# Hybrid trunk, attention stage: the rest of a pair's query and key projection is asked for one head sooner in the order

## The chip, the cores and the metric

One core of a Trainium2 chip runs the whole program. The metric is the device time of one execution in microseconds (us). The kernel before takes 1062.12 us (median of 3 runs, 1062.06 to 1062.16). The profile comes from an execution of its own, with its own time.

## The reference

Two residual layers on 512 tokens of width 1024, all in float32. Each has a mixer and then an MLP, with an RMSNorm ahead of both; a last norm ends it.

```
h = x
layer 0:  h += attention(rmsnorm(h)) @ w_o        # 16 heads of 64, 8 chunks of 64 tokens
          h += relu(rmsnorm(h) @ w1)**2 @ w2      # hidden 4096
layer 1:  h += recurrent_block(rmsnorm(h))        # conv, gates, linear scan
          h += relu(rmsnorm(h) @ w1)**2 @ w2
out = rmsnorm(h) * norm_final

attention: q, k, v = h @ w_qkv
           s = q @ k.T / 8 + bias[head][clip(i - j)]     # own chunk and the 8 before it
           o = softmax(s) @ v
```

The change touches the attention of layer 0 alone. With 512 tokens the band of nine chunks covers all earlier tokens, so scores are computed in four blocks of 128 queries against 128, 256, 384 and 512 keys.

## The kernel before, in words

*Precision.* Every product of two float32 matrices is done as three matmuls of rounded parts (`mm3`): the operand is split into a high part, a copy in the narrower format, and a low part, the operand minus that copy; high x high, high x low and low x high are added. So each weight tile that is loaded (`wr`) costs a copy on ScalarE (`wh`, line 140) and a subtraction on VectorE (`wl`, line 143) before TensorE can use it.

*Weights.* `plan` lists every weight tile in the order of use. `want(n)` hands out the next n and asks for loads up to four tiles ahead. Five split tiles can be alive at once, three raw ones. All loads go through SP's queue.

*Attention.* The heads are worked in pairs, pair p being heads 2p and 2p+1. The projections of pairs 0 and 1 come first, with the norm. The rest is done head by head in the loop of line 539: in iteration i the scores of head i (`score`, tile `s` on lines 408 and 409, eight matmuls), the transposes of head i-1's probabilities (`turn`, tile `x`, line 439, ten), and the weighing of values of head i-2 (`weigh`, tile `oa`, lines 454 and 455, eight). Between a head's scores and its transposes lies its softmax: on VectorE the addition of the bias with a maximum (line 412), on ScalarE the exponentials (line 419), on VectorE a reciprocal and the scaling (lines 423 and 426).

*Projection steps as filling.* The projections of the later pairs (`q2`, `k2`, ... `q7`, `k7`), the values (`v0`, `v1`) and the output projection (`wo...`) stand in one queue of generators, in this order: v0, q2, k2, q3, k3, q4, k4, v1, q5, k5, q6, k6, q7, k7, then the output projection. One step is three matmuls (one `mm3`) and costs two credits. `fill(7.6)` gives 7.6 credits, with at most 3 kept from before, and runs steps while the credit is above zero; it stands behind `score`, behind `turn` and behind `weigh`. An item may only start in a fill once a certain head's scores have been written (for pair p, head 2p-3). `need(name)` runs steps until the named item is finished, whatever the credit, which may fall far below zero; later fills then do nothing until it is paid back.

At the end of an item stands its output. For a key projection this is `k_out`: a scaling on VectorE (tile `tk`, line 316), then for each head of the pair a copy on ScalarE (`kh`, line 321), a subtraction on VectorE (`kl`, line 322) and two small DMAs on SP's queue that copy both to the other 64 partitions (lines 323 and 324), since the scores multiply the low and the high part of a query in one matmul. `q_out` (lines 304 to 312) is alike without the DMAs.

*Buffers.* Eight PSUM banks: four with the tag "mm" (projections, `oa`), four with the tag "at", of which a head's scores take three and a head's transposes three. Query and key tiles have two buffers per head of a pair, so that pair p+2 reuses those of pair p. The bias of four heads (`bias_of`, line 295) has one buffer: its load on SP's queue (line 297), four copies and a fill on POOL (lines 299 and 300).

*Order.* The source gives no order per engine. The framework that builds the program takes the source's order as the rank of each instruction, estimates when its operands and its buffer will be there, and writes each engine's queue from that; where the higher-ranked instruction would not be ready, a later-ranked one is put ahead. On the chip every engine then runs its queue in that order and waits where an operand is late.

The lines that set the order around the change:

```
        def fill(n):
            credit[0] = min(credit[0], 3) + n
            while credit[0] > 0 and queue and at[queue[0][2][0]] >= queue[0][2][1]:
                step()

        for i in range(NH + 2):
            if i < NH:
                ...
                if i >= 4:
                    need(f"k{i // 2}")
                score(i)
```

Of the kernel before, what the change touches and what calls it, by code (L numbers as in the profile page):

```python
# [40 lines left out]
def trunk(ctx: ExitStack, tc: tile.TileContext, xT, cols, gfin, win, wqkv, wo, rwin, rga, rgx, rwo, w1, w2, out):  # L41
# [21 lines left out]
    def residual(name):  # L63
        both = [per.tile([P, 4, T], F32, name=f"{name}{i}", tag=f"hx{i}") for i in range(2)]
        hT[:] = [both[k // 4][:, k % 4] for k in range(KT)]
        hT2[:] = [both[k // 2][:, 2 * (k % 2) : 2 * (k % 2) + 2] for k in range(4)]
# [221 lines left out]
    with ExitStack() as actx:  # L288
# [6 lines left out]
        def bias_of(g):  # L295
            b = ab.tile([P, 4, T], F32, name=f"bias{g}", tag="bias")
            nc.sync.dma_start(b[:, :, 2 * P :], win[4 * g : 4 * g + 4].rearrange("h p j -> p h j"))
            for h in range(4):
                G.tensor_copy(b[:, h, 0 : 2 * P], b[:, h, 2 * P : 2 * P + 1].to_broadcast([P, 2 * P]))
            G.memset(b[0:HD, :, T - HD :], NEG)  # L300
            biases[g] = b
# [96 lines left out]
        def score(h):  # L398
            kh, kl = kk[h]
            s0, s1, s2 = atp(f"s0{h}"), atp(f"s1{h}"), atp(f"s2{h}")  # L400
            sc = [s0[:, 0:P], s0[:, P : 3 * P], s1[:, : 3 * P], s2]
            pt = a2.tile([P, 10 * P], F32, name=f"p{h}", tag="p")
            mx = a2.tile([P, 4], F32, name=f"mx{h}", tag="mx")
            sm = a2.tile([P, 4], F32, name=f"sm{h}", tag="sm")
            b = biases[h // 4]
            for t in range(4):
                n = (t + 1) * P
                PE.matmul(sc[t], q[h][:, t * P : n], kl[:, :n], start=True, stop=False)
                PE.matmul(sc[t], q[h][:, t * P : n], kh[:, :n], start=False, stop=True)  # L409
            for t in range(4):  # L410
                n = (t + 1) * P
                V.tensor_tensor_reduce(  # L412
                    out=pt[:, seg[t] : seg[t] + n], in0=sc[t], in1=b[:, h % 4, T - n :],
                    scale=1.0, scalar=-3.0e38, op0=ALU.add, op1=ALU.max, accum_out=mx[:, t : t + 1],
                )
            V.tensor_scalar(mx, mx, -1.0, None, ALU.mult)  # L416
            for t in range(4):
                n = (t + 1) * P
                S.activation(  # L419
                    pt[:, seg[t] : seg[t] + n], pt[:, seg[t] : seg[t] + n], AF.Exp,  # L420
                    bias=mx[:, t : t + 1], accum_out=sm[:, t : t + 1],
                )
            V.reciprocal(sm, sm)
            for t in range(4):
                n = (t + 1) * P
                V.tensor_scalar(pt[:, seg[t] : seg[t] + n], pt[:, seg[t] : seg[t] + n], sm[:, t : t + 1], None, ALU.mult)
            pts[h] = pt

        def turn(h):
            pt = pts.pop(h)  # L430
            x0, x1, x2 = atp(f"x0{h}"), atp(f"x1{h}"), atp(f"x2{h}")
            dst = {(0, t): (x0, t * P) for t in range(4)}
            dst.update({(1, t): (x1, (t - 1) * P) for t in range(1, 4)})
            dst.update({(2, t): (x2, (t - 2) * P) for t in range(2, 4)})
            dst[3, 3] = (x1, 3 * P)
            for kt in (0, 1, 3, 2):
                for t in range(kt, 4):
                    b, c = dst[kt, t]
                    PE.transpose(b[:, c : c + P], pt[:, seg[t] + kt * P : seg[t] + (kt + 1) * P], ident)  # L439
            pH = a2.tile([P, 10 * P], F32R, name=f"pH{h}", tag="pH")  # L440
            pL = a2.tile([P, 10 * P], F32R, name=f"pL{h}", tag="pL")
            for b, c, n in ((x0, 0, T), (x1, T, T), (x2, 2 * T, 2 * P)):
                S.copy(pH[:, c : c + n], b[:, :n])  # L443
                V.tensor_sub(pL[:, c : c + n], b[:, :n], f(pH[:, c : c + n]))
            pHL[h] = (pH, pL)

        def weigh(h):
            pH, pL = pHL.pop(h)
            p, hh = h // 2, h % 2
            oa = mmp(f"oa{h}")  # L450
            for kt in range(4):
                c, n = pseg[kt]
                vv = vt[p // 2][:, kt, p % 2, 2 * hh : 2 * hh + 2, :].rearrange("p s d -> p (s d)")
                PE.matmul(oa[:, T - n :], vv, pL[:, c : c + n], start=kt == 0, stop=False)
                PE.matmul(oa[:, T - n :], vv, pH[:, c : c + n], start=False, stop=kt == 3)
            own, oth = HALF[hh], HALF[1 - hh]
            if hh == 0:
                oT[p] = a2.tile([P, T], F32, name=f"o{p}", tag="o", bufs=1)
            ax = a2.tile([P, T], F32, name=f"ax{h}", tag="ax", bufs=1)
            S.copy(ax[own], oa[oth])  # L460
            V.tensor_add(oT[p][own], oa[own], ax[own])
            if hh == 1:
                oH = ao.tile([P, T], F32R, name=f"oH{p}", tag="oH")
                oL = ao.tile([P, T], F32R, name=f"oL{p}", tag="oL")
                S.copy(oH, oT[p])
                V.tensor_sub(oL, oT[p], f(oH))
                oHL[p] = (oH, oL)
# [54 lines left out]
        def step():  # L522
            try:
                credit[0] -= next(queue[0][1])
            except StopIteration:
                queue.pop(0)
# [6 lines that stand above are left out]
        def need(name):  # L533
            while any(name == item[0] for item in queue):
                step()
# [3 lines left out]
        for i in range(NH + 2):  # L539
            if i < NH:  # L540
                if i % 4 == 0 and i > 0:
                    bias_of(i // 4)
                if i >= 4:
                    need(f"k{i // 2}")
                score(i)
                at["s"] = i
            fill(FILL)
            if 0 <= i - 1 < NH:
                turn(i - 1)
            fill(FILL)  # L550
            if 0 <= i - 2 < NH:
                if i == 15:
                    need("woA")
                need(f"v{(i - 2) // 8}")
                weigh(i - 2)
                if i == 9:
                    residual("h")
                    for k in range(KT):
                        nc.sync.dma_start(hT[k], xT[k * P : (k + 1) * P, :])
                at["w"] = i - 2  # L560
            fill(FILL)
# [478 lines left out]
```

## Time and profile before

| | |
|---|---|
| median of 3 runs | 1062.12 us |
| the profiled execution | 1062.76 us, span of its instructions 1060.7 us |
| TensorE (PE) | 1051.2 us busy, 99% of the span, 4820 matmuls |
| weight loads (PEld), beside the matmuls | 870.6 us, 82% |
| VectorE (DVE) | 798.6 us, 75% |
| ScalarE (ACT) | 586.9 us, 55% |
| DMA | 111.51 MB, 105 GB/s on average |
| granted TensorE clock | 0.999 |

An engine's busy time is the sum of its instructions' durations. Matmuls overlap in the engine: their starts are recorded, their ends are modelled, so a matmul that is shown with 0.39 us may be followed by the next one after 0.23 us. PEld rows are weight loads, which run beside the matmul before. A row of the timeline that ends in a bracket tells how long the engine stood idle before it, and what it waited for. Tiles are named without their numbers, so `s` is the score tile of any head; which head it is follows from the order of the rows. The attention stage with its output projection lies between about 36 and 240 us.

### The profile page before, as it was taken

The numbers are of one execution on the slowest core, as the hardware profiler recorded it, in microseconds if no ns is written. First come the engines' busy times: TensorE is split into PE (matmuls) and PEld (weight loads), VectorE is DVE, ScalarE is ACT, GpSimd is POOL, SyncE is SP. The second block draws the span as 40 slices with busy tenths as digits, with TensorE's granted clock in tenths as the row PEclk, the third lists the DMA queues.
The fourth block names the chain that finished last, engine by engine and source line by source line (L and its number), as shares of the span: only waits on it lengthen the run. The fifth ranks groups of instructions, "written<-read, shape, count | busy, mean of one in ns | idle before, by whom it ended". The sixth has DMA issues, their size and how long they took to land.

```text
span 1060.7 us, 12851 instructions
## 1 busy us (share of the span) xinstructions
PE 1051.2 (99%) x4820; PEld 870.6 (82%) x4820; DVE 798.6 (75%) x1176; ACT 586.9 (55%) x888; POOL 8.8 (1%) x28
## 2 busy tenths in 40 slices
PE   9999999999999999999999999999999999999997
PEld 7888888888888888888888878888888888888886
DVE  6798779867395697587599799984387487577596
ACT  6677557645464554454456587555454454454454
POOL 0000000000000000000000000000000000000000
PEclk9999999999999999999999999999999999999999
DMA  8444353255046036026103222283136126125002
GB/s 263 117 124 135 80 168 110 70 164 164 21 121 192 6 96 202 21 80 198 40 0 118 84 77 88 71 286 92 40 87 201 31 80 198 40 79 179 1 1 80
DMA packets 128414, 111.51 MB, mean 105 GB/s; under 512 B 4321, under 2 KB 104673, under 8 KB 128353
## 3 DMA queue, kind: packets, MB, share of 16 engines
q1 hardware_dynamic: 127776, 109.99, 33.9%
q8 instruction: 38, 0.62, 0.2%
q10 hardware_dynamic: 576, 0.72, 0.2%
q14 instruction: 24, 0.19, 0.1%
HBM read 104.39 MB, written 2.10 MB: 100 GB/s over the span
## 4 chain that ended last, share of the span: by engine, by line
PE 93%; DVE 2%; DMA 2%; ACT 1%; issue 1%; SPq 0%; ACTq 0%; DVEq 0%
PE u L217 11%; PE u L219 11%; PE u L218 11%; PE x L219 5%; PE x L218 5%; PE x L217 5%; PE y L217 3%; PE y L218 3%; PE y L219 3%; PE x L439 2%; PE wo L217 1%; PE wo L218 1%; PE ro L219 1%; PE ro L217 1%; PE xb L217 1%; PE wo L219 1%
## 5 line engine op out<-in xcount | busy, mean ns | idle before, releaser
L143 DVE TENSOR_TENSOR wl<-wr,wh 128x1024 fp32r<-128x1024 f32 (+1 forms) x122 | 146.5, 1203 | 94.7 <-ACT wh L140 90.0
L140 ACT CAST wh<-b 128x1024 fp32r<-128x1024 f32 x112 | 117.8, 1052 | 177.2 <-PE u L218 130.9
L140 ACT CAST wh<-wr 128x1024 fp32r<-128x1024 f32 (+1 forms) x121 | 125.7, 1039 | 140.6 <-PE u L218 66.1
L143 DVE TENSOR_TENSOR wl<-b,wh 128x1024 fp32r<-128x1024 f32 x112 | 136.6, 1219 | 87.7 <-ACT wh L140 87.6
L217 PE MATMUL u<-hnH,wh 128*128 128x512 f32 x512 | 200.1, 391 | 0.0
L219 PE MATMUL u<-hnH,wl 128*128 128x512 f32 x512 | 199.4, 389 | 0.0
L218 PE MATMUL u<-hnL,wh 128*128 128x512 f32 x512 | 199.2, 389 | 0.0
L219 PEld LDWEIGHTS u<-hnH,wl 128*128 128x128 f32 x512 | 96.1, 188 | 20.2
L218 PEld LDWEIGHTS u<-hnL,wh 128*128 128x128 f32 x512 | 96.2, 188 | 19.8
L217 PEld LDWEIGHTS u<-hnH,wh 128*128 128x128 f32 x512 | 96.1, 188 | 19.7
L138 DVE TENSOR_TENSOR b<-b,b 128x1024 f32<-128x1024 f32 x64 | 76.3, 1216 | 1.8 <-DMA b<-in_w 1.5
L217 PE MATMUL x<-wh,h 128*128 128x512 f32 x128 | 50.0, 391 | 0.0
L218 PE MATMUL x<-wl,h 128*128 128x512 f32 x128 | 49.9, 390 | 0.0
L641 ACT ACTIVATE a<-u 128x512 f32<-128x512 f32 x64 | 37.8, 591 | 13.3 <-PE u L219 13.3
L629 DVE SCALAR_TENSOR_TENSOR d<-x,rq,d 128x512 f32<-128x512 f32 x60 | 42.8, 743 | 0.5 <-PE x L219 0.5
L642 ACT ACTIVATE a<-a 128x512 f32<-128x512 f32 x64 | 40.6, 635 | 1.8
L419 ACT ACTIVATE p<-p,mx 128x128 f32<-128x128 f32 (+1 forms) x64 | 35.2, 552 | 6.2 <-DVE mx L416 6.0
L662 ACT CAST h<-a 128x1024 fp32r<-128x1024 f32 (+2 forms) x34 | 27.2, 800 | 6.7 <-PE y L218 5.7
L412 DVE CUSTOM_DVE_ANT_0 p<-s,bias 128x128 f32<-128x128 f32 (+1 forms) x64 | 27.7, 484 | 3.4 <-PE s L409 3.1
L443 ACT CAST pH<-x 128x512 fp32r<-128x512 f32 (+1 forms) x48 | 21.7, 517 | 13.7 <-PE x L439 13.5
L218 PEld LDWEIGHTS x<-wl,h 128*128 128x128 f32 x128 | 24.0, 188 | 4.9
L217 PEld LDWEIGHTS x<-wh,h 128*128 128x128 f32 x128 | 24.0, 188 | 4.9
(342 smaller groups left out, 2290.5 us busy)
## 6 DMA issues: line engine op xcount, KB each, us to landing
wr<-in_w SPq DMA_DIRECT2D x64, 512.0 KB, 3.9
b<-in_w SPq DMA_DIRECT2D x64, 512.0 KB, 4.3
wr<-in_wqkv SPq DMA_DIRECT2D x20, 512.0 KB, 3.9
wr<-in_rwin SPq DMA_DIRECT2D x16, 512.0 KB, 3.4
wr<-in_wo SPq DMA_DIRECT2D x8, 512.0 KB, 4.0
wr<-in_rwo SPq DMA_DIRECT2D x8, 512.0 KB, 3.4
x<-in_xT SPq DMA_DIRECT2D x8, 256.0 KB, 4.6
bias<-in_win SPq DMA_DIRECT2D x4, 512.0 KB, 4.6
```

The costliest lines, as they stand in the source:

```text
L138: V.tensor_sub(raw, raws[x, half], raws[y, half])
L140: S.copy(H[:, :n], raw[:, :n])
L143: low = V.tensor_sub(L[:, :n], raw[:, :n], f(H[:, :n]))
L217: PE.matmul(acc, WH, XH, start=start, stop=False, skip_group_check=more)
L218: PE.matmul(acc, WH, XL, start=False, stop=False, skip_group_check=more)
L219: PE.matmul(acc, WL, XH, start=False, stop=stop, skip_group_check=more)
L412: V.tensor_tensor_reduce(out=pt[:, seg[t] : seg[t] + n], in0=sc[t], in1=b[:, h % 4, T - n :], scale=1.0, scalar=-3.0e38, op0=ALU.add, op1= ...
L419: S.activation(pt[:, seg[t] : seg[t] + n], pt[:, seg[t] : seg[t] + n], AF.Exp, bias=mx[:, t : t + 1], accum_out=sm[:, t : t + 1],)
L629: V.scalar_tensor_tensor(d, acc, r, d, ALU.mult, ALU.add)
L641: S.activation(c, acc.rearrange("p (h c) -> p h c", h=2), AF.Relu)
L642: S.activation(c, c, AF.Square)
L662: S.copy(H[:, ks], raw[n][:, ks])
```

## The change

In iteration i of the loop the projection of the next pair's keys (and with it everything ahead of it in the queue) is finished before the scores of an odd head already: `need` names pair (i+1)//2, from head 3 on and at most pair 7, where it named pair i//2 from head 4 on. So pair p is finished ahead of the scores of head 2p-1 and no longer ahead of those of head 2p. The steps that `need` runs spend credit, and later fills run fewer.

```
--- before.py
+++ after.py
@@ -540,8 +540,8 @@
             if i < NH:
                 if i % 4 == 0 and i > 0:
                     bias_of(i // 4)
-                if i >= 4:
-                    need(f"k{i // 2}")
+                if i >= 3:
+                    need(f"k{min((i + 1) // 2, 7)}")
                 score(i)
                 at["s"] = i
             fill(FILL)
```

## Rows read from the trace of the kernel before

**Rows 1.** The page: span, and busy time, share and instructions of TensorE.
```profile
span 1060.7 us, 12851 instructions
...
PE 1051.2 (99%) x4820; PEld 870.6 (82%) x4820; DVE 798.6 (75%) x1176; ACT 586.9 (55%) x888; POOL 8.8 (1%) x28
```

**Rows 2.** Busy time by stretch: length, each engine's us (instructions), clock, DMA share, GB/s.
```profile
36.00:60.00 24.00, 23.72 (x122) 19.52 (x121) 19.63 (x58) 17.92 (x44) 0.00 (x0) 1.00 0.30 80
60.00:100.00 40.00, 39.56 (x206) 33.29 (x204) 36.12 (x89) 26.45 (x63) 2.54 (x5) 1.00 0.45 122
100.00:160.00 60.00, 60.00 (x312) 51.17 (x311) 47.87 (x119) 36.70 (x84) 1.68 (x5) 1.00 0.46 136
160.00:240.00 80.00, 79.80 (x407) 66.47 (x405) 66.59 (x150) 48.51 (x106) 1.97 (x5) 1.00 0.38 117
300.00:400.00 100.00, 100.00 (x443) 82.78 (x442) 75.03 (x103) 51.84 (x63) 0.00 (x0) 1.00 0.35 106
```

**Rows 3.** Waits of TensorE, whole span: us in total, times, longest.
```profile
PE s L408 <- DMA kl<-kl: 0.4, 1, 0.4
PE s L408 <- DVE v L354: 0.3, 1, 0.3
```

**Rows 4.** TensorE in order of time, end of k2 to head 4's transposes.
```profile
74.77 0.39 PE L219 MATMUL qk2k_out<-hnH,wl 128*128 128x512 f32 x1
75.00 0.39 PE L217 MATMUL qk3q_out<-hnH,wh 128*128 128x512 f32 x1
75.23 0.39 PE L218 MATMUL qk3q_out<-hnL,wh 128*128 128x512 f32 x1
...
80.58 0.40 PE L218 MATMUL qk3q_out<-hnL,wh 128*128 128x512 f32 x1
81.42 0.30 PE L408 MATMUL s<-kl,q 128*128 128x128 f32 x1 [0.44 <-DMA kl<-kl]
...
82.79 1.25 PE L439 MATMUL x<-ident,p 128*128 128x128 f32 x10
83.80 0.48 PE L219 MATMUL qk3q_out<-hnH,wl 128*128 128x512 f32 x1
...
89.50 1.21 PE L439 MATMUL x<-ident,p 128*128 128x128 f32 x9
```

**Rows 5.** TensorE in order of time, end of k5 to head 10's scores.
```profile
152.30 0.39 PE L219 MATMUL qk5k_out<-hnH,wl 128*128 128x512 f32 x1
152.53 0.40 PE L454 MATMUL oa<-pL,v 128*128 128x512 f32 x1
...
153.75 0.45 PE L217 MATMUL qk6q_out<-hnH,wh 128*128 128x512 f32 x1
...
157.91 0.39 PE L217 MATMUL qk6q_out<-hnH,wh 128*128 128x512 f32 x1
158.14 0.22 PE L408 MATMUL s<-kl,q 128*128 128x128 f32 x1
```

**Rows 6.** VectorE in order of time: k2's output, first reductions of heads 4 and 12.
```profile
75.66 0.69 DVE L316 TENSOR_TENSOR tk<-qk2k_out,n0acc 128x512 f32<-128x512 f32 x1
...
78.42 1.40 DVE L322 TENSOR_TENSOR kl<-tk,kh 64x512 fp32r<-64x512 f32 x2
...
82.26 0.29 DVE L412 CUSTOM_DVE_ANT_0 p<-s,bias 128x128 f32<-128x128 f32 x1 [0.41 <-PE s L409]
...
180.17 0.28 DVE L412 CUSTOM_DVE_ANT_0 p<-s,bias 128x128 f32<-128x128 f32 x1
```

**Rows 7.** SP's issues (the bias load, k2's copies) and POOL's last bias steps, by time.
```profile
67.91 0.37 SPq L297 DMA_DIRECT2D bias<-in_win  x1
...
74.31 0.30 POOL L300 MEMSET bias<- 64x256 f32 x1
...
79.12 1.18 SPq L324 DMA_DIRECT2D kl<-kl  x2
...
169.55 0.30 POOL L300 MEMSET bias<- 64x256 f32 x1
```

**Rows 8.** Waits of ScalarE's weight splits, 36 to 216 us: total, times, longest.
```profile
ACT wh L140 <- PE qk5k_out L218: 2.5, 1, 2.5
...
ACT wh L140 <- PE qk4k_out L218: 1.7, 1, 1.7
```

**Rows 9.** Landing times of the four bias loads, from issue.
```profile
DMA to landing us min/median/max: 3.7/4.6/6.2
```

More of the change, by code (lines that the diff above doesn't have):

```diff
@@ L542, in trunk @@
                     bias_of(i // 4)
-                if i >= 4:
-                    need(f"k{i // 2}")
+                if i >= 3:
+                    need(f"k{min((i + 1) // 2, 7)}")
                 score(i)
```

## The prediction

> **What bounds the kernel now.** I read the page's first two parts, then the waits of TensorE, then the busy time by stretches, and only then single instructions around the moved work.
>
> TensorE is busy for 1051.2 us of a span of 1060.7 us [rows 1]. The stretches show the same for the attention stage: between 36 and 240 us it stands still for 0.28 + 0.44 + 0.00 + 0.20 = 0.92 us, and VectorE, the next engine, works 170.2 of those 204 us [rows 2]. The list of waits names the two pieces of size: 0.3 us on VectorE, and 0.4 us on the DMA that copies a half of kl (a key's low part) to the other partitions [rows 3]. The second is the one the change speaks to: it falls before head 4's scores, the first scores of pair 2 [rows 4].
>
> A busy figure alone would not do, since ends of matmuls are modelled. Starts are not: a 512-column matmul follows the one before by 0.22 to 0.23 us [rows 4], and 443 of them fill the 100 us of the MLP between 300 and 400 us, 0.226 us each [rows 2]. So the attention stage runs at the pace of a stage that has no stalls, at a granted clock of 1.00, and what a reordering can give back is what stands idle, 0.92 us.
>
> The reader should also see that TensorE does not run the source's order. In the source nothing stands between the last step of k2 and head 4's scores. In the trace k2 ends with the matmul at 74.77 us, scores follow at 81.42 us, and the 6.4 us between are full: q3 from 75.00 us on, without a gap up to the last 0.44 us [rows 4]. At head 10 it is alike: the last k5 matmul is at 152.30 us, the scores are at 158.14 us, and between stand eight matmuls of a weigh step and 19 of q6, which the source puts behind them [rows 5]. Whoever writes the order per engine takes the source as a ranking and puts later projection steps where an operand is not ready.
>
> **The change part by part.** It adds and removes no instruction: the same 4820 matmuls, the same copies. It ranks the rest of pair p's projection ahead of the scores of head 2p-1 instead of 2p. I counted the steps by hand from the credit rule (7.6 credits per fill, 2 per step): ahead of head 3's scores now come 13 steps (5 of q2, 8 of k2), of head 5's 7, of head 7's none but k4's output, of head 9's 25 (9 of v1, then q5 and k5), of head 11's 16, of head 13's 11. A step is three matmuls of 0.227 us, 0.68 us. From head 14 on the ranking is as before.
>
> Matmuls: total unchanged, so 0.
>
> The wait on kl: 0.44 us [rows 4]. From k2's last matmul the chain runs: output at 75.66 us, low parts from 78.42 us [rows 6], copies of kl issued from 79.12 us [rows 7], scores at 81.42 us [rows 4], so 6.65 us from the start of that matmul. Afterwards one whole head (scores 82.79 - 81.42 = 1.37 us, transposes 83.80 - 82.79 = 1.01 us [rows 4], weigh 153.75 - 152.53 = 1.22 us [rows 5], together 3.6 us) lies between by rank alone, and q3 can fill the other 3 us. So up to 0.44 us goes. It may equally come back, because the order is made to an estimate that was 0.44 us too early here. Bounds: -0.44 to 0; I take -0.44.
>
> What is late next: VectorE and ScalarE get the four output operations of a projection before a softmax instead of after it. VectorE does 36.1 us of work in the 40 us from 60 to 100 us [rows 2], so softmaxes of the odd heads move later, those of the even heads earlier. On TensorE this shows as new waits of the kind that are there already. Bounds: below, all of the 0.92 us goes, which is 0.48 beyond the 0.44; above, the bare heads of the first rival. The nearest row is the mean of the two waits of [rows 3], 0.36 us; I take one of these, +0.36 us.
>
> The queues: SP gets the four copies kh, kl one head sooner, ahead of the bias load of heads 4 to 7 in the source. They wait for ScalarE and VectorE while weight loads stand behind them. Their cover is the stock of split weights: ScalarE's weight splits wait for TensorE to release a buffer (2.5 us at k5, 1.7 us at k4) [rows 8], so weights lie ready and are not what is late. 0. POOL's part is in the second rival.
>
> Sum: -0.44 + 0.36 = -0.08 us. The profiled execution took 1062.76 us, 2.1 us around its span of 1060.7 us, and lies 0.64 us above the median of 1062.12 us; the difference is applied to the median: 1062.04, so **1062.0 us**.
>
> One rule speaks against reading the stage as full. The Trainium skill, in Perfetto Trace Analysis, section Identifying the Most-Contended Engine, says that TensorE's matmul occupancy is a poor sign of how close a kernel is to its limit and that weight-load time should be read instead. By that rule TensorE is at 82% here, 870.6 us [rows 1]; what it would give is the last rival.
>
> **The rivals.** *The bare heads.* If the engines kept the source's order, two heads would have no projection step beside them. By the credits the fills after head 9 and head 10, and those around head 11, are empty. From scores to transposes of one head takes 89.50 - 81.42 = 8.08 us [rows 4]; between them would stand scores, transposes, weigh and the next scores, 1.37 + 1.01 + 1.22 + 1.37 = 4.97 us. So 3.1 us of waiting at heads 9 and 11 each, 1.7 at head 3 (two q3 steps beside it), 0.4 at head 13 (four steps): 8.3 us, and 1062.12 - 0.44 + 8.3 = 1070.0 us. For it: this is what the code says. Against it: by the same sum the old order would wait 1.7 us at head 10, and from 100 to 160 us TensorE never stands, from 160 to 240 us for 0.2 us [rows 2].
>
> *The bias load becomes the late one: slower.* There is one bias buffer. The load for heads 4 to 7 may start only when head 3's scores are reduced: it goes at 67.91 us [rows 7], and POOL has it ready at 74.31 + 0.30 = 74.61 us [rows 7], 7.65 us before head 4's first reduction at 82.26 us, which waits for TensorE and not for it [rows 6]. Head 3's scores now rank 13 steps, 8.85 us, later. If head 4 keeps its place, the bias comes at 83.46, 1.2 us late. The load for heads 12 to 15 is ready at 169.86 us [rows 7]; 16 steps later is 180.78, 0.6 us after head 12's first reduction at 180.17 us [rows 6]. Behind these reductions TensorE's transposes wait for the banks. With one of the loads at its longest, 6.2 instead of 4.6 us to land [rows 9], the price is 1.2 + 0.6 + 1.6 = 3.4 us, and 1062.12 - 0.44 + 3.4 = 1065.1 us. It decides as soon as it costs more than 0.44 us, and passes 0.2% from 2.6 us on. Against it: 6.4 us of q3 were put into the like gap at head 4 [rows 4], and each pair's 16 steps, 10.9 us, are free to go there.
>
> *The ranking changes, the time does not.* k2 already ended 6.65 us ahead of its scores; if they are again set to the estimated landing, the 0.44 us stays: 1062.1 us. For it: in [rows 5] the k5 copies were met with no wait at all, so one miss in six may be chance.
>
> *Room behind the busy time: faster.* If the matmuls of the stage could be drawn to the pace of their weight loads, 36 to 240 us would shrink by PE less PEld, 4.2 + 6.3 + 8.8 + 13.3 = 32.6 us [rows 2], to 1029.5 us. Against it: the MLP has the same ratio, 82.78 of 100 us [rows 2], and nothing here touches a matmul's columns.
>
> **How the numbers follow.** Forecast 0.62, the unchanged time 0.19, bias 0.12, bare heads 0.04, room 0.01, and 0.02 for a gain of all idle time (1061.2 us). 0.2% is 2.1 us, about what a measurement of this kernel can tell from no change. Faster by more needs over twice the idle time of the stage, so it has the room's 0.01 and 0.02 for what I have not seen: 0.03. Slower by more is 0.09 of the bias case (0.03 of it stays under 2.6 us), the bare heads' 0.04 and 0.01 unseen: 0.14. The rest, 0.83, is the same. The range begins at 1061.2 us, with all 0.92 us gone, and ends at 1064.3 us, three quarters of the way from the forecast to the bias case: that leaves out some 0.04 below and 0.13 above.
>
> **What would show it.** Right: the wait of scores on the kl copy gone from TensorE's list; head 3's scores behind k2's last matmul, some 9 us later in the order; head 4's scores at most 4 us after the copies land, with q3 matmuls ahead of them; TensorE's idle time between 36 and 240 us below 1.5 us; the waits on VectorE 0.2 to 0.8 us. Bias: VectorE's reduction of head 4 or 12 waits for POOL, and transposes on it. Bare heads: gaps of 2 to 3 us before the transposes of heads 9 and 11. The prediction is wrong if that idle time passes 3 us, or if stalls appear beyond 240 us, where the source is the same.

## The result, and the profile after

The changed kernel takes **1066.61 us** (median of 6 runs, 1065.16 to 1066.94) against 1061.87 us for the kernel before (6 runs): ratio 1.0042, 95% interval 1.0032 to 1.0052. It is 4.7 us slower. The forecast was 1062.0 us in a range of 1061.2 to 1064.3 us, with a chance of 0.14 for slower by more than 0.2%. A second set of five runs gave 1066.61 us again, ratio 1.0043 (1.0030 to 1.0055).

The page of the profiled execution (1065.16 us, the shortest of the six), as in [rows 1]:

```profile
span 1063.4 us, 12837 instructions
...
PE 1051.4 (99%) x4820; PEld 870.2 (82%) x4820; DVE 799.1 (75%) x1176; ACT 588.3 (55%) x888; POOL 9.4 (1%) x28
```

TensorE's work is the same, 1051.4 against 1051.2 us. The time went into standing still, and into one stage. Busy time by stretch, the answer to [rows 2]:

```profile
36.00:60.00 24.00, 24.00 (x124) 19.88 (x122) 19.40 (x61) 17.71 (x47) 0.00 (x0) 1.00 0.31 80
60.00:100.00 40.00, 39.26 (x203) 32.60 (x202) 35.92 (x90) 25.80 (x58) 2.13 (x5) 1.00 0.49 142
100.00:160.00 60.00, 58.94 (x306) 49.99 (x305) 47.44 (x117) 38.15 (x89) 2.06 (x5) 1.00 0.40 116
160.00:240.00 80.00, 77.67 (x394) 64.44 (x393) 63.13 (x143) 46.21 (x100) 1.67 (x5) 1.00 0.36 105
```

The idle time is the length less the first number behind it: 0.00, 0.74, 1.06 and 2.33 us, 4.13 us in all where 0.92 us stood before. The granted clock is 1.00 in each stretch, so none of it is clock. The spans of the two traces differ by 2.7 us only, because the traced run of before waited 0.84 us for its first weights and 0.28 us at head 0, and this one did not; such waits in the first 45 us come and go between runs of one order (the second trace of the changed kernel has 0.99 us at head 0). A measure free of them is the stretch from head 2's first score matmul to the MLP's first matmul. Its two ends, in the kernel before and then in the changed one (in the second line of each: shortest, median and longest duration, first and last start):

```profile
52.65 0.22 PE L408 MATMUL s<-kl,q 128*128 128x128 f32 x1
...
L217 PE MATMUL u<-hnH,wh x512: 389/389/486, 246.0 to 1020.4; 128*128 128x512 f32 x171
```

```profile
50.75 0.22 PE L408 MATMUL s<-kl,q 128*128 128x128 f32 x1
...
L217 PE MATMUL u<-hnH,wh x512: 389/389/486, 248.4 to 1023.0; 128*128 128x512 f32 x171
```

193.4 us became 197.6 us, 4.3 us more (197.4 us in the second trace), with the same 983 matmuls; this I call the stage below. It is more than the idle time shows (from 45 to 240 us 4.13 us, in the kernel before 0.64 us, so 3.49 more). The reason is in the next rows: a wait is counted from the modelled end of the matmul ahead of it.

The waits of TensorE from 30 to 240 us, as in [rows 3]:

```profile
PE x L439 <- DVE p L426: 1.3, 3, 0.6
PE x L439 <- DVE mx L412: 0.9, 1, 0.9
PE oa L454 <- DVE pL L444: 0.9, 1, 0.9
PE s L408 <- DMA kl<-kl: 0.8, 1, 0.8
```

Where there were two there are six, and no longer at head 4. By place, with two short ones that the list leaves out: at head 3's transposes 0.64 and 0.09 us, head 8's weighing 0.87, head 9's transposes 0.19, head 10's weighing 0.13, head 12's scores 0.80, head 11's transposes 0.95, head 13's transposes 0.46 us. TensorE in order of time around heads 8 and 9, and at head 11:

```profile
147.36 0.39 PE L219 MATMUL qk5k_out<-hnH,wl 128*128 128x512 f32 x1
147.58 0.22 PE L408 MATMUL s<-kl,q 128*128 128x128 f32 x1
...
148.86 1.25 PE L439 MATMUL x<-ident,p 128*128 128x128 f32 x10
149.87 0.48 PE L454 MATMUL oa<-pL,v 128*128 128x512 f32 x1
...
152.21 0.50 PE L454 MATMUL oa<-pL,v 128*128 128x512 f32 x1 [0.87 <-DVE pL L444]
152.54 0.39 PE L455 MATMUL oa<-pH,v 128*128 128x512 f32 x1
152.77 0.40 PE L217 MATMUL qk6q_out<-hnH,wh 128*128 128x512 f32 x1
...
177.83 0.40 PE L218 MATMUL qk7q_out<-hnL,wh 128*128 128x512 f32 x1
179.17 0.66 PE L439 MATMUL x<-ident,p 128*128 128x128 f32 x4 [0.95 <-DVE mx L412]
```

The reader is to see three things. First, k5 runs without a break up to head 9's scores, and then scores (head 9), transposes (head 8), weighing (head 7) and weighing (head 8) follow with no projection step between: 2.5 us after head 8's transposes began, at 151.34 us, their low parts are asked for, and they are not there for another 0.87 us. Second, q6, which waits for nothing, stands right behind the waiting instruction: this fits an order written for an estimate by which the low parts would be ready (the estimate itself was not read). Third, from 177.83 to 179.17 us are 1.34 us where 0.23 us are usual, so that wait cost 1.11 us and not 0.95: the modelled end hides 0.16 us of it. The Trainium skill, in Perfetto Trace Analysis, section Tensor Engine Instruction (MATMUL, LD_WEIGHTS), says that the profiler reports an end that is estimated and not observed. The trace agrees, by 0.16 us at this wait.

VectorE in order of time beside it:

```profile
148.94 0.55 DVE L412 CUSTOM_DVE_ANT_0 p<-s,bias 128x384 f32<-128x384 f32 x1
149.42 0.08 DVE L412 DVE_READ_ACCUMULATOR2_ANT mx<- 128x1 f32 x1
149.42 1.40 DVE L322 TENSOR_TENSOR kl<-tk,kh 64x512 fp32r<-64x512 f32 x2
150.85 0.69 DVE L412 CUSTOM_DVE_ANT_0 p<-s,bias 128x512 f32<-128x512 f32 x1
151.47 0.08 DVE L412 DVE_READ_ACCUMULATOR2_ANT mx<- 128x1 f32 x1
151.47 0.69 DVE L444 TENSOR_TENSOR pL<-x,pH 128x512 fp32r<-128x512 f32 x1
```

The key output of pair 5 (`kl`, 1.40 us) now falls between the third and the fourth reduction of head 9, and head 8's low parts (`pL`) come behind all of them. At head 12 a third thing joins, the bias buffer. SP, POOL and VectorE by time:

```profile
170.18 2.47 SPq L324 DMA_DIRECT2D kl<-kl  x2
170.68 0.69 DVE L412 CUSTOM_DVE_ANT_0 p<-s,bias 128x512 f32<-128x512 f32 x1
...
172.76 0.53 SPq L297 DMA_DIRECT2D bias<-in_win  x1
...
178.13 0.30 POOL L300 MEMSET bias<- 64x256 f32 x1
...
178.47 0.29 DVE L412 CUSTOM_DVE_ANT_0 p<-s,bias 128x128 f32<-128x128 f32 x1 [1.66 <-POOL bias L300]
```

Head 11's last reduction (170.68 us), put off by pair 6's `kl` too, frees the bias buffer; the load goes out behind the four copies on SP's queue, POOL is done at 178.43 us, head 12's first reduction waits 1.66 us for it, and head 11's transposes, which need the bank it reads, wait 0.95 us on TensorE. In the kernel before, that reduction came 10.3 us after the bias was ready [rows 6, 7].

### The profile page after: what moved, and what is told of

Its sections match the earlier page's. It is cut to its first block, busy times and chain, and to the rows that moved or that the text cites. A ratio compares the mean times of both kernels' runs of the same rounds, so it can differ in the third digit from the quotient of the medians.

```text
span 1063.4 us, 12837 instructions
## 1 busy us (share of the span) xinstructions
PE 1051.4 (99%) x4820; PEld 870.2 (82%) x4820; DVE 799.1 (75%) x1176; ACT 588.3 (55%) x888; POOL 9.4 (1%) x28
## 4 chain that ended last, share of the span: by engine, by line
PE 94%; DVE 3%; DMA 1%; issue 1%; ACT 0%; POOL 0%; POOLq 0%; SPq 0%; ACTq 0%; DVEq 0%
PE u L217 11%; PE u L219 11%; PE u L218 11%; PE x L218 5%; PE x L217 5%; PE x L219 5%; PE y L217 3%; PE y L219 3%; PE y L218 3%; PE ro L219 1%; PE ro L217 1%; PE v L217 1%; PE xb L217 1%; PE xb L218 1%; PE xb L219 1%; PE v L218 1%
## 5 line engine op out<-in xcount | busy, mean ns | idle before, releaser
L419 ACT ACTIVATE p<-p,mx 128x128 f32<-128x128 f32 (+1 forms) x64 | 35.2, 551 | 10.4 <-DVE mx L416 10.3
```

The lines of the kernel that those rows point to most:

```text
L419: S.activation(pt[:, seg[t] : seg[t] + n], pt[:, seg[t] : seg[t] + n], AF.Exp, bias=mx[:, t : t + 1], accum_out=sm[:, t : t + 1],)
```

## The experiments

Theory A: with the steps run ahead of an odd head's scores, nothing is left to stand between the stages of this head and its neighbours, and each such place waits. Theory B: the key output among the odd head's reductions delays its softmax. Theory C: the one bias buffer. Each run below is set against the kernel before on the same chip (median 1061.8 to 1062.1 us). A first trial was the changed kernel itself once more:

> The changed kernel once more, for a second trace and as the mark that the other runs of this set are measured against. All theories: 1.0042 of the kernel before (1.0032 to 1.0052), about 1066.4 us; TensorE idle 4.1 us between 36 and 240 us (3.5 to 5), in the same places as in the first trace: ahead of head 3's, 9's, 11's and 13's transposes, head 8's weighing and head 12's scores.

1066.61 us, 1.0043 (1.0030 to 1.0055). The same places, with 0.62, 0.07, 0.86, 0.19, 0.13, 0.44, 1.22 and 0.45 us: they belong to the order, not to the run.

**The output late, the steps early.** The steps are counted, and the odd head's demand stops ahead of the output:

```
-                if i >= 3:
-                    need(f"k{min((i + 1) // 2, 7)}")
+                if i >= 4:
+                    need(f"k{i // 2}")
+                if i >= 3 and i % 2 and i < NH - 1:
+                    name = f"k{(i + 1) // 2}"
+                    while any(name == item[0] for item in queue) and done.get(name, 0) < KT:
+                        step()
```

> The changed kernel, but a pair's key output (scaling, splits, copies) ranks where it did before the change; the matmul steps alone stand one head sooner. Theory A (close heads: with the matmul steps spent ahead of an odd head, its scores, transposes and weighing and those of its neighbours follow one another within some 5 us, and every joint is a place to wait): the steps are still spent, so the waits stay, 1065.3 to 1067 us, idle 3 to 5 us. Theory B (the key output falls among the odd head's reductions on VectorE and ScalarE and delays its softmax by 2 to 3.5 us): the waits at heads 8 to 9 go, 1062 to 1064 us, idle under 2 us. Theory C (the bias load): no difference from the changed kernel.

1064.62 us, 1.0029 (1.0018 to 1.0039), between A's range and B's. Head 8's weighing waits 0.11 us and not 0.87, head 13's transposes 0.07 and not 0.46, those of heads 3 and 11 not at all, and VectorE no longer waits for POOL's bias: with the output in its old rank these go. But head 9's transposes wait 0.62 us where they waited 0.19, and the other waits have moved to the next scores. TensorE from 30 to 240 us:

```profile
PE s L408 <- DMA kl<-kl: 2.4, 2, 1.3
...
PE x L439 <- DVE p L426: 0.6, 1, 0.6
```

Heads 4 and 12 stand 1.14 and 1.27 us for the copies of kl, the wait that the change was to remove, since the steps that covered it are spent. So neither rank of the output is free.

**Steps that cost no credit.**

```
                 if i >= 3:
+                    kept = credit[0]
                     need(f"k{min((i + 1) // 2, 7)}")
+                    credit[0] = kept
```

> The changed kernel, but the steps that are run ahead of the scores cost no credit, so that the fills behind those scores still run steps of the projections that come next. Theory A: odd heads have matmuls beside them again, the idle time falls below 2 us and the time to 1062 to 1064 us; new waits may come late in the stage, when the queue has run out sooner. Theory B: the output still falls among the reductions, 1065 to 1067 us. Theory C: no difference, 1066.4 us.

1062.19 us, 1.0003 (0.9994 to 1.0012): all of it is back. The stage is 193.6 us long. TensorE after head 9's scores, and VectorE:

```profile
148.91 0.39 PE L409 MATMUL s<-kh,q 128*128 128x512 f32 x1
149.14 0.40 PE L217 MATMUL qk6q_out<-hnH,wh 128*128 128x512 f32 x1
...
151.21 1.25 PE L439 MATMUL x<-ident,p 128*128 128x128 f32 x10
152.22 0.48 PE L217 MATMUL qk6q_out<-hnH,wh 128*128 128x512 f32 x1
...
155.05 0.39 PE L454 MATMUL oa<-pL,v 128*128 128x512 f32 x1
```

```profile
149.71 1.40 DVE L322 TENSOR_TENSOR kl<-tk,kh 64x512 fp32r<-64x512 f32 x2
151.14 0.69 DVE L412 CUSTOM_DVE_ANT_0 p<-s,bias 128x512 f32<-128x512 f32 x1
```

Nine matmuls of q6 stand behind the scores and twelve behind the transposes, and nothing waits there. The `kl` of 1.40 us is between the same two reductions as in the changed kernel: where steps stand beside, it costs nothing. That is against B by itself. What waits are left are new ones, 0.77 us amid head 5's scores and 0.55 us amid head 11's.

**The bias taken away.** One bias for all heads, on the changed kernel and, as a control, on the kernel before; this leaves out the three later bias loads and POOL's work on them:

```
-            b = biases[h // 4]
+            b = biases[0]
...
-                if i % 4 == 0 and i > 0:
-                    bias_of(i // 4)
```

> The changed kernel with the bias of heads 0 to 3 used for all heads: leaves out the three later bias loads and POOL's copies of them. Theory C (head 4's and 12's reductions come too early for the one bias buffer): 2 us or more come back, 1064.4 us or less. Theories A and B: only the 0.28 us go that VectorE waited for POOL at head 4, 1065.5 to 1066.8 us.

1063.87 us, 1.0020 (1.0012 to 1.0029), 2.7 us less than the changed kernel: C's number. Head 11's transposes no longer wait; the 0.88 us of head 8, 0.65 of head 3, 0.48 at head 12 (0.80 and 0.44 in the two traces of the changed kernel) and 0.46 of head 13 stay.

> The kernel before with the bias of heads 0 to 3 used for all heads: leaves out the three later bias loads and POOL's copies. The control for the same edit on the changed kernel, which took 2.7 us off it. If the bias load is late only in the changed order (theory C for its share), this is the kernel before, 1061.3 to 1062.2 us. If leaving the loads out is worth something by itself (DMA or SP time for the weights), it is 1059 to 1060.5 us.

1061.45 us, 0.9992 (0.9983 to 1.0001). So of the 2.7 us some 0.7 us come from the loads left out, by the interval anything from none to 1.8 us; about 2 us are left for the bias buffer.

**The bias in two buffers of two heads**, with all its work:

```
-            b = ab.tile([P, 4, T], F32, name=f"bias{g}", tag="bias")
+            b = ab.tile([P, 2, T], F32, name=f"bias{g}", tag="bias", bufs=2)
...
-                if i % 4 == 0 and i > 0:
-                    bias_of(i // 4)
+                if i % 2 == 0 and i > 0:
+                    bias_of(i // 2)
```

> The changed kernel with all its work, but the bias kept in two buffers of two heads instead of one of four (the same memory): the load for heads 12 and 13 waits for head 9's reductions and not for head 11's. Theory C for its share: head 12's reductions wait no longer for POOL and head 11's transposes no longer on them; like the kernel with one bias, 1063.2 to 1064.4 us. If that one gained from the loads it left out, this stays at 1066 us or more.

1064.88 us, 1.0027 (1.0016 to 1.0038): 1.7 us back, VectorE waits no longer for POOL, and head 11's transposes stand 0.24 us and not 0.95. It lies 0.5 us above the range of C. Head 12's scores wait 0.18 us (0.80 and 0.44 in the changed kernel's traces), head 3's transposes 0.86 us and not 0.64; the rest of the waits is as in the changed kernel.

**The low part of the keys on POOL.**

```
-                V.tensor_sub(kl[own], tmp[own], f(kh[own]))
+                G.tensor_sub(kl[own], tmp[own], f(kh[own]))
```

> The changed kernel with the low part of the keys subtracted on POOL instead of VectorE (1.4 us per pair leave VectorE, which the trace shows between the third and the fourth reduction of heads 3, 9 and 11). Theory B: those heads' softmax starts 1.4 us sooner, the waits before their transposes and head 8's weighing shrink, 1064 to 1065.5 us; the copies may come later instead, since POOL is slower. Theory A: 1066 to 1067 us.

1071.03 us, 1.0083 (1.0070 to 1.0097): both theories missed. POOL takes 1.28 us for the first half of a pair and 2.14 us for the second, where VectorE takes 0.69 for either, and VectorE becomes slower while POOL works (last section). TensorE's longest wait in this stage:

```profile
PE oa L454 <- DVE pL L444: 2.1, 1, 2.1
```

Behind it the granted clock fell, as in the stage of no other trace (last section). The stage is 202.6 us long, 5.0 us more than in the changed kernel: 2.7 us of it are idle time, and some 1.7 us, by an estimate, the clock. As a test between A and B it says nothing.

**Half the steps.** On the kernel before, the query alone one head sooner:

```
                 if i >= 4:
                     need(f"k{i // 2}")
+                if i >= 3:
+                    need(f"q{min((i + 1) // 2, 7)}")
```

> The kernel before, with the query projection alone asked for one head sooner; the key projection is asked for where it was. Half the steps move and the key output stays. Theory A: about half the waits, 1063 to 1064.8 us. Theories B and C: no key output among an odd head's reductions, and the odd head's last reduction is not put off by it, so close to the kernel before, 1061.5 to 1062.8 us.

1063.85 us, 1.0018 (1.0009 to 1.0027), in A's range and outside that of B and C, though no key output is moved. (The query's output is moved with its steps, so this speaks against the key output, not against every output among the reductions.) Its waits are of the same kind: copies of kl 1.1 us (heads 12 and 14), transposes of head 10 0.64 us.

**One demand alone.** On the kernel before, `if i in (9,)` (or `(11,)`) with `need(f"k{(i + 1) // 2}")`:

> The kernel before with the early demand at head 9 alone: 9 steps of v1 and the 16 of pair 5 stand ahead of head 9's scores, all other demands are as before. Theory A with the places of the changed kernel's trace: the waits ahead of head 8's weighing (0.87 us) and head 9's transposes (0.19 us), each with some 0.16 us that the modelled end of a matmul hides, and none elsewhere: 1062.8 to 1064 us. If the waits of the changed kernel come from the sum of its demands, and not from each place, this is the kernel before, 1061.3 to 1062.5 us.

1063.04 us, 1.0008 (0.9999 to 1.0017), in A's range. Head 8's weighing waits 0.86 us, head 9's transposes 0.19 us, as in the full change; a wait of 0.25 us is new at head 12.

> The kernel before with the early demand at head 11 alone (16 steps). Theory A and the bias share of theory C: waits ahead of head 10's weighing, head 12's scores and head 11's transposes, 1.9 us shown and some 0.5 us hidden, with VectorE waiting for POOL's bias at head 12: 1063.5 to 1065 us. If only the sum of the demands counts: 1061.3 to 1062.5 us.

1063.41 us, 1.0014 (1.0005 to 1.0022), a little under A's range: head 10's weighing 0.24 us, head 12's scores 0.67, head 11's transposes 0.32, and VectorE waits 0.86 us for POOL's bias at head 12. The two add up to 1.0 + 1.3 = 2.3 of the 4.7 us, with the waits of the full change at their heads. The rest, from the demands at heads 3 to 7 and 13 and from what the demands do to one another, was not run alone.

**The credit given back at some heads alone**, `credit[0] = kept if i in (9, 11) else credit[0]`, and its counterpart with `not in`:

> The changed kernel with the credit given back at heads 9 and 11 alone. Theory A: the waits at these two places go, in the changed kernel's trace ahead of head 8's weighing, head 9's transposes, head 10's weighing, head 12's scores and head 11's transposes, 2.9 us shown and some 0.8 us hidden by modelled ends; those at heads 3 and 13 stay: 1062.3 to 1063.6 us. If the key output among the reductions sets it (theory B), it is still there at heads 9 and 11, and the time stays at 1065.5 us or more.

1063.75 us, 1.0014 (1.0005 to 1.0023). All waits at heads 8 to 12 are gone, and that of head 13 with them; head 3's stay (0.65 and 0.09 us), and a new one of 1.38 us stands amid head 11's scores. That puts the time 0.15 us above A's range and far below B's.

> The changed kernel with the credit given back at all early demands but those of heads 9 and 11 (heads 3 to 8, 10 and 12 to 15). Theory A: the counterpart: the waits at heads 3 and 13 go, 1.2 us shown and some 0.5 us hidden, those at heads 9 and 11 stay as far as there are still steps ahead of these heads: 1064 to 1065.7 us. Theory B: 1065.5 us or more.

1063.90 us, 1.0018 (1.0010 to 1.0027), just under A's range. Heads 3 and 13 wait no longer, heads 9 and 11 do (0.66, 0.21 and 0.59 us), and the new wait at head 5 is that of the kernel without charge. Each set of heads loses its own waits when its fills come back. But each loses some of the other's too (head 13's in the first; those of head 8's and head 10's weighing and of head 12's scores in the second), since credit that is given back moves all later steps: the waits are tied to the missing steps, but not head by head.

**Both remedies, and the buffers alone.** Two versions that might have beaten the kernel before: the changed kernel without charge and with the split bias, and the kernel before with the split bias.

> The changed kernel with both remedies: early steps that cost no credit, and the bias in two buffers of two heads. With the credit remedy alone no wait on the bias is left in the trace, so the buffers should add nothing: 1061.4 to 1062.6 us. If the bias load still sets when heads 4, 8 and 12 can go, some 0.5 us less: 1060.7 to 1061.3 us, and a version that beats both.

1062.60 us, 1.0005 (0.9995 to 1.0014).

> The kernel before with the bias in two buffers of two heads. Its trace shows no wait on the bias, so nothing should come of it: 1061.5 to 1062.5 us. The two loads more could push weight loads back on SP's queue: then up to 1063 us.

1062.56 us, 1.0004 (0.9995 to 1.0012). (Eight loads stand here for four, so four more and not two.) Neither is faster; no version with all its work beat the kernel before.

## Why the prediction was wrong

- *The matmuls unchanged, 0*: right (1051.4 us).
- *The wait on kl at head 4, -0.44 us*: it went from head 4 as said, but one of 0.80 us stands at head 12, where besides the stages of heads 9 to 11 only four matmuls of q7 are left ahead of the scores.
- *What is late next, +0.36 us*: this is the step that failed. It measured 4.13 us shown, or some 4.7 us by the stage: 4.3 us more and 0.44 us that were saved. I had taken one wait of the size seen before, since the rows of heads 4 and 10 showed projection steps put into the gaps [rows 4, 5]. But those gaps were of 6 us, ahead of scores that need the key output. The new waits are of 0.1 to 1.2 us, at places that the order treats as ready (inferred from the order; the estimate was not read). What covered such places before was the slack that the rank gave: head 8's weighing began 16.7 us after its transposes (135.82 to 152.53 us), now it is due after 2.5 us and begins after 3.35 us.
- *The bare heads* were the right mechanism in the right places, dismissed at 0.04 because TensorE does not keep the source's order. Priced at 1.7, 3.1, 3.1 and 0.4 us for heads 3, 9, 11 and 13, they measured 0.73, 1.06, 1.88 and 0.46 us shown, 4.13 against 8.3 us: the filling took half. That the old order had not waited at head 10 was true and no proof for the new one. By the credits head 10 was as bare there, with k5's output ahead of its scores. But its scores need that output, so 19 matmuls of q6 were put in between [rows 5], and the output was done by then. Head 9's scores do not need k5: they follow its last matmul at once (147.36 and 147.58 us), and the output falls among their reductions.
- *The bias* was right at head 12 (0.6 us late foretold, 1.66 measured) and small at head 4 (1.2 foretold, 0.28 measured). "6.4 us of q3 were put into the like gap" failed in the same way, and was misread: the gap holds 20 matmuls of q3 and, from 79.08 to 80.30 us, the eight of head 2's weighing. The bias makes up some 2 of the 4.7 us, with the two rivals meeting in one place: head 11 is bare, so nothing covers its transposes while they wait for the bias.
- *SP's and ScalarE's queues, 0*: right for the weights; no wait on a weight was seen. But the four copies on SP stood ahead of the bias load, which the prediction names and gives no price: head 11's last reduction ended at 171.4 us, the load went at 172.76 us.
- The text's own mark for being wrong, more than 3 us of idle time between 36 and 240 us, was passed with 4.13 us.

What stays open is how much each of the two causes would cost with the other one gone: the key output explains which stage is late, the missing steps that it is waited for, and the runs do not give them separate prices. The estimate by which the order is written was not read, so how far it is off at these places is not shown. What stands behind the stage also differs by 0.25 us between the two traces (814.97 and 814.72 us), which no run here explains.

## What to carry to other kernels

A unit that is busy for 99% of the time bounds what a reordering can win, never what it can lose. Independent work that is asked for sooner is taken away from the place where it stood: list what it covered there, and price each joint that becomes bare by the trace's own chain from producer to consumer, even where a planner fills gaps: here it filled those ahead of scores that need the moved output, and left the short ones. Ask above all whether the stage that now stands behind the moved work needs it: head 9's scores did not, so nothing was put between, and the output fell into their own softmax. A resource with one buffer (here the bias) belongs into that list with the instruction that frees it and the queue behind which its load stands.

## What was not expected of the hardware

With the keys' low part on POOL, VectorE in order of time, while POOL worked from 152.48 to 155.98 us:

```profile
152.48 3.50 POOL L322 TENSOR_TENSOR kl<-tk,kh 64x512 fp32r<-64x512 f32 x2 [27.34 <-ACT kh L321]
...
153.25 1.60 DVE L143 TENSOR_TENSOR wl<-wr,wh 128x1024 fp32r<-128x1024 f32 x1
154.78 1.23 DVE L416 TENSOR_SCALAR mx<-mx 128x4 f32<-128x4 f32 x1
```

The weight split took 1.60 us where it takes 1.23 us, and the negation of four columns 1.23 us where the changed kernel has 0.16 us. The reductions and the low parts `pL`, which read one operand from SBUF and one from PSUM, kept their 0.69 and 0.68 us beside POOL. The Trainium skill, in SBUF — State Buffer, section Who interferes with whom, says that an instruction of VectorE that reads two SBUF inputs, or runs in a two-port mode, and one of POOL that reads SBUF exclude each other for their whole length. The trace agrees: the four-column instruction stands for 1.23 us and ends at 156.0 us, with POOL's second half. By this an offload to POOL is priced with what VectorE loses beside it.

The second thing is TensorE's clock in the same run. From 157.03 to 160.44 us the granted clock was 0.5, the lower of its two levels (1.2 and not 2.4 GHz), and 512-column matmuls of the scores followed at 0.43 us and not at 0.23. Just before, TensorE had run head 8's transposes and head 7's weighing and then stood for 2.38 us from start to start (2.10 us shown) for head 8's low parts. Half speed for 3.41 us costs some 1.7 us, by this estimate. In the stage of every other trace the granted clock stayed at 1.00.
